# Moving the pool of split tiles behind the pool of small tiles, which changes its address modulo 512

## The chip, the cores and the metric

One core of one Trainium2 chip runs the whole program. The metric is the device time of one execution in microseconds, as the median of several runs.

## The reference

The program is a four-layer encoder on 256 tokens of width 1024, float32 throughout:

```python
for i in range(DEPTH):                        # 4 layers
    h = rmsnorm(x, norm_mix_g[i])
    h = mixer(h)                              # layer 0: SSD, 1: dilated attention, 2: differential attention, 3: SSD
    x = x + h
    x = x + jnp.square(jax.nn.relu(rmsnorm(x, norm_mlp_g[i]) @ w1[i])) @ w2[i]   # 1024 -> 4096 -> 1024
return rmsnorm(x, final_norm_g)
```

Nearly all the work is in products of the 256 tokens with weight matrices that are read once each (HBM reads are 296 MB in all).

## The kernel before, in words

**Products.** Activations lie transposed, 128 channels by 256 tokens to a tile. A product with weights is done at the fast matmul rate by splitting both factors: a hi part that is the float32 rounded to `float32r`, and a lo part, the rest. `mm3` (lines 144 to 151) then issues three matmuls into one place of PSUM. Each loads a 128x128 piece of weights into the array and streams an activation tile of 128x256 past it (the moving operand):

```python
mm(out, lhsT=wh, rhs=xh, start=start, stop=False, skip_group_check=True)   # L149
mm(out, lhsT=wh, rhs=xl, start=False, stop=False, skip_group_check=True)   # L150
mm(out, lhsT=wl, rhs=xh, start=False, stop=stop, skip_group_check=True)    # L151
```

A few weights stay whole (`native`); L147 multiplies them as plain float32 with the tile `nf`.

**Weights.** `pump` brings them in chunks of 128x1024: SP issues the DMA into `raw` (5 buffers), ScalarE copies the hi part into `whi` (L110), VectorE writes the rest into `wlo` (L112), 5 buffers each. The order of the chunks is planned ahead, and `done` lets the pump run on when TensorE is through with a chunk.

**Moving operands.** There are three families. `split_tile` (line 217) gives tiles `spl`, two 128x256 blocks each, from a ring of 12 in the pool `sp`; they outlive a layer and hold the split input of an MLP, of a mixer's first units (`norm_split`, L232 and L233) and the split inputs of the output projections. The tiles `nh` and `nl` (pool of the layer) hold the normalised input of a mixer, and `hh` and `hl` (pool of the layer) the hidden activations of an MLP.

**An MLP** (`mlp`, from line 325) goes over eight slices of 512 hidden channels. `up(s)` takes four chunks and multiplies them with all eight `spl` blocks, 96 matmuls into two `r` banks; `evac` squares and splits the result into `hh` and `hl`; `down(s - 1)` takes four chunks and multiplies them with `hh` and `hl`, 96 matmuls into the four `a` banks. `norm_finish` stands after the first `up`. So in each MLP 768 matmuls stream `spl` and 768 stream `hh` or `hl`, in turns of 96.

**The mixers** interleave their units by numbers in tables (`CFG`, `DIL`, `DIFF`). Their input projections stream `nh` and `nl`; the first units of each (`defer`) and all output chunks (`out_chunk`, `proj_tail`) stream `spl`. In the two SSD mixers these are 2 x 480 matmuls, in the dilated one 336, in the differential one 288. In the dilated mixer each pair of heads has two streams of `qk` (48 and 96 matmuls on `nh`) between its other work. In the differential mixer the V projection (L972 to L974) loads `nh` into the array and streams `whi` and `wlo`; its scores (L130, L131) load `q` and stream `k` and `kl`.

**Where things lie.** Pools are laid out one behind another in the order in which `Prog.__init__` makes them, each tile with its ring of buffers. Byte addresses in a partition of the built program:

| pool | tiles | begins | modulo 512 |
|---|---|---|---|
| `wp` | `raw`, then `whi`, then `wlo`, 5 x 4096 bytes each | 32032 (`whi` 52512, `wlo` 72992) | 288 |
| `sp` | 12 `spl` of 2048 bytes | 93472 | 288 |
| `small` | six of 32 bytes, nine of 1024 (`rbc`, `dg`, `sqacc`, `sq`): 9408 bytes | 118048 | `rbc` and later 480 |
| layer | `hh`, `hl`, or `nh`, `nl` first | 127456 | 480 (`nh`, `nl` of the dilated mixer 480 too) |

All buffers of `whi`, `wlo`, `spl`, `hh`, `nh` step by a multiple of 512 bytes, and a 128x128 piece of weights is 512 bytes wide, a moving block 1024; so all pieces of a family have the same address modulo 512. In the differential mixer `k` and `kl` begin at 0 modulo 512, and `q` too.

Of the kernel before, what the change touches and what calls it, by code (L numbers as in the profile page):

```python
# [35 lines left out]
class LayerPool:  # L36


    def __init__(self, prog):
        self.prog = prog  # L40
# [5 lines left out]
class Prog:  # L46
    def __init__(self, ctx, tc, aps, parts):
        self.ctx, self.tc, self.nc, self.a = ctx, tc, tc.nc, aps
        self.parts = parts
        ep = lambda name, bufs=1, **k: ctx.enter_context(tc.tile_pool(name=name, bufs=bufs, **k))  # L50
        self.const = ep("const")
        self.xp = ep("xp")
        self.wp = ep("wp")
        self.sp = ep("sp")
        self.ap_ = ep("small")
        self.lp = None
        self.dr = ep("dr", space=bass.MemoryType.DRAM)
        self.ps = ep("ps", space=PSUM)
        self.head = self.const.tile([P, aps["head"].shape[1]], F32, name="head")
        self.vec = self.const.tile([P, aps["vec"].shape[1]], F32, name="vec")  # L60
        self.cst = self.const.tile([P, aps["cst"].shape[1]], F32, name="cst")
        self.plan = []
        self.rep, self.bvec = {}, None
        self.n_dma = self.n_conv = self.n_take = self.n_done = 0
        self.chunks = {}
# [1206 lines left out]
```

## Time and profile before

| | |
|---|---|
| median of 3 runs | 1622.55 us (1619.86 to 1624.77) |
| the profiled execution | 1627.18 us, its span 1625.4 us |
| granted clock of TensorE, mean over the span | 0.987 |
| HBM read | 296.41 MB, 185 GB/s over the span |

The span lies between the first and the last instruction. A busy time of TensorE in the profile is the union of its matmuls' lengths; these overlap, so the length of one isn't what it costs. What it costs in a stream that does not wait is the step from its start to the start of the next, which the view of single instructions in order of time shows.

### The profile page before, as it was taken

Reading aid. Unit: us, or ns where it says so; the run is one execution under the profiler, and the core shown is the slowest. Engines: PE = TensorE matmul, PEld = TensorE weight load, DVE = VectorE, ACT = ScalarE, POOL = GpSimd, SP = SyncE. Lnnn points to the kernel's source line nnn. Section 1 sums busy time; section 2 is a strip of 40 time slices with the busy share of each in tenths; the row PEclk is TensorE's granted clock in tenths of the full one; section 3 lists DMA queues with packets and bytes.
Section 4 is the critical chain, followed back from the end, with each engine's and each line's share of the span. In section 5 each row is a group of like instructions: output and inputs, shape, how many; then the busy total and the mean of one; then the engine's idle time right before and its main releaser. Section 6 shows DMA issues by size and latency. Waiting matters only on the chain.

```text
span 1625.4 us, 32385 instructions
## 1 busy us (share of the span) xinstructions
PE 1594.5 (98%) x13018; PEld 1550.6 (95%) x13018; DVE 1194.8 (74%) x1996; ACT 959.2 (59%) x1627; POOL 132.9 (8%) x122
## 2 busy tenths in 40 slices
PE   8999999999999999999999999999999999999998
PEld 7989999999989999999999999999999899899997
DVE  6999997555777667666556898755579999985554
ACT  5577865444657666655445677544455777654443
POOL 0012121000200000010000100100010232210001
PEclk9999999999999999999999999999999999999999
DMA  6668755765465556546665564566656677656661
GB/s 209 220 211 240 227 193 178 222 211 184 137 179 161 168 156 170 170 141 184 186 191 183 177 200 133 179 193 184 187 144 199 210 218 222 212 174 184 193 184 64
DMA packets 230294, 299.84 MB, mean 184 GB/s; under 512 B 16496, under 2 KB 166256, under 8 KB 230144
## 3 DMA queue, kind: packets, MB, share of 16 engines
q1 hardware_dynamic: 209552, 262.51, 53.0%
q10 hardware_dynamic: 20592, 35.27, 7.5%
q8 instruction: 102, 1.67, 0.4%
q14 instruction: 48, 0.39, 0.1%
HBM read 296.41 MB, written 3.62 MB: 185 GB/s over the span
## 4 chain that ended last, share of the span: by engine, by line
PE 80%; DVE 10%; DMA 4%; ACT 3%; issue 2%; POOL 0%; SPq 0%; DVEq 0%; ACTq 0%; POOLq 0%
PE r L149 14%; PE r L151 14%; PE r L150 14%; PE a L149 8%; PE a L150 8%; PE a L151 8%; DVE wlo L112 3%; PE r L147 2%; DMA raw<-in_ssd_in_w_dram 2%; PE a L829 1%; PE a L828 1%; PE a L830 1%; DMA bc<-scr 1%; PE r L620 1%; PE a L887 1%
## 5 line engine op out<-in xcount | busy, mean ns | idle before, releaser
L112 DVE TENSOR_TENSOR wlo<-raw,whi 128x1024 fp32r<-128x1024 f32 (+1 forms) x490 | 592.1, 1216 | 307.2 <-ACT whi L110 306.7
L110 ACT CAST whi<-raw 128x1024 fp32r<-128x1024 f32 (+1 forms) x490 | 502.5, 1032 | 459.4 <-PE r L150 244.1
L151 PE MATMUL r<-spl,wlo 128*128 128x256 f32 x1248 | 357.4, 287 | 4.0 <-DVE wlo L112 4.0
L149 PE MATMUL r<-spl,whi 128*128 128x256 f32 x1248 | 359.0, 288 | 0.6 <-ACT whi L110 0.5
L150 PE MATMUL r<-spl,whi 128*128 128x256 f32 x1248 | 358.1, 287 | 0.3 <-DVE spl L233 0.3
L149 PE MATMUL r<-nh,whi 128*128 128x256 f32 (+1 forms) x1024 | 291.2, 284 | 5.4 <-DVE kl L142 3.7
L151 PE MATMUL r<-nh,wlo 128*128 128x256 f32 (+1 forms) x1024 | 285.9, 279 | 0.7 <-DVE wlo L112 0.7
L150 PE MATMUL r<-nl,whi 128*128 128x256 f32 (+1 forms) x1024 | 286.0, 279 | 0.0
L149 PE MATMUL a<-hh,whi 128*128 128x256 f32 x1024 | 283.3, 277 | 0.0
L150 PE MATMUL a<-hl,whi 128*128 128x256 f32 x1024 | 283.1, 276 | 0.0
L151 PE MATMUL a<-hh,wlo 128*128 128x256 f32 x1024 | 282.6, 276 | 0.0
L151 PEld LDWEIGHTS r<-spl,wlo 128*128 128x128 f32 x1248 | 243.0, 195 | 4.5 <-DVE wlo L112 4.4
L149 PEld LDWEIGHTS r<-spl,whi 128*128 128x128 f32 x1248 | 243.1, 195 | 1.3 <-ACT whi L110 1.0
L150 PEld LDWEIGHTS r<-spl,whi 128*128 128x128 f32 x1248 | 243.1, 195 | 0.9 <-DVE spl L233 0.5
L149 PEld LDWEIGHTS r<-nh,whi 128*128 128x128 f32 (+1 forms) x1024 | 193.0, 188 | 9.1 <-issue 5.4
L151 PEld LDWEIGHTS r<-nh,wlo 128*128 128x128 f32 (+1 forms) x1024 | 193.0, 188 | 1.7 <-DVE wlo L112 0.9
L150 PEld LDWEIGHTS r<-nl,whi 128*128 128x128 f32 (+1 forms) x1024 | 193.6, 189 | 0.7 <-DVE nl L306 0.2
L149 PEld LDWEIGHTS a<-hh,whi 128*128 128x128 f32 x1024 | 192.3, 188 | 0.2 <-ACT whi L110 0.2
L150 PEld LDWEIGHTS a<-hl,whi 128*128 128x128 f32 x1024 | 192.4, 188 | 0.0
L151 PEld LDWEIGHTS a<-hh,wlo 128*128 128x128 f32 x1024 | 192.2, 188 | 0.0
L246 POOL TENSOR_TENSOR sqacc<-sqacc,sq 128x256 f32<-128x256 f32 x48 | 43.0, 896 | 1111.6 <-ACT sq L244 1110.1
L595 ACT ACTIVATE e<-bc,tb 128x256 f32<-128x256 f32 (+1 forms) x256 | 95.5, 447 | 2.1 <-issue 1.7
(249 smaller groups left out, 2412.9 us busy)
## 6 DMA issues: line engine op xcount, KB each, us to landing
raw<-in_mlp_w_dram SPq DMA_DIRECT2D x256, 512.0 KB
raw<-in_ssd_in_w_dram SPq DMA_DIRECT2D x96, 512.0 KB
bc<-scr ACTq DMA_DIRECT2D x32, 768.0 KB
raw<-in_dil_qkv_w_dram SPq DMA_DIRECT2D x48, 512.0 KB
raw<-in_ssd_out_w_dram SPq DMA_DIRECT2D x32, 512.0 KB
raw<-in_dil_qkv_w_dram SPq DMA_DIRECT2D x64, 192.0 KB
raw<-in_diff_qkv_w_dram SPq DMA_DIRECT2D x24, 512.0 KB
raw<-in_dil_out_w_dram SPq DMA_DIRECT2D x8, 512.0 KB
```

Of the source, the lines that this page charges most:

```text
L110: self.nc.scalar.copy(out=hi[:, :n], in_=raw[:, :n])
L112: self.nc.vector.tensor_tensor(out=lo[:, :n], in0=raw[:, :n], in1=hi[:, :n].bitcast(F32), op=ALU.subtract)
L147: mm(out, lhsT=wh, rhs=xh, start=start, stop=stop, skip_group_check=True)
L149: mm(out, lhsT=wh, rhs=xh, start=start, stop=False, skip_group_check=True)
L150: mm(out, lhsT=wh, rhs=xl, start=False, stop=False, skip_group_check=True)
L151: mm(out, lhsT=wl, rhs=xh, start=False, stop=stop, skip_group_check=True)
L246: nc.gpsimd.tensor_tensor(out=self.sqs[0], in0=self.sqs[0], in1=sq, op=ALU.add)
L595: X = lambda o, i_, bias: nc.scalar.activation(out=o, in_=i_, func=AF.Exp, bias=bias)
L620: nc.tensor.matmul(b[(h % 2) * 64:(h % 2) * 64 + 64, n * T:(n + 1) * T], lhsT=xt[:, 1 - i, h * 64:(h + 1) * 64], rhs=G[h][:, i * T:(i + 1) ...
L828: mm(o, lhsT=nh[:, k, t], rhs=w_h, start=k == 0, stop=False)
L829: mm(o, lhsT=nh[:, k, t], rhs=w_l, start=False, stop=False)
L830: mm(o, lhsT=nl[:, k, t], rhs=w_h, start=False, stop=k == 7)
```

## The change

The pool `small` is made ahead of the pool `sp`, so it takes the place right behind the weights.

```diff
         self.wp = ep("wp")
+        self.ap_ = ep("small")
         self.sp = ep("sp")
-        self.ap_ = ep("small")
         self.lp = None
```

In the built program `small` now begins at 93472 and `sp` at 102880; everything else lies where it was. Each `spl` is 9408 bytes higher (18 x 512 + 192, so 480 modulo 512), each small tile 24576 bytes lower (48 x 512, the same modulo 512). The instructions of every engine, their order and what they wait for are the same in both programs, row by row.

## Rows read from the trace of the kernel before

**Rows 1.** Page, part 1: busy us of each engine (share of the span) xinstructions.

```profile
PE 1594.5 (98%) x13018; PEld 1550.6 (95%) x13018; DVE 1194.8 (74%) x1996; ACT 959.2 (59%) x1627; POOL 132.9 (8%) x122
```

**Rows 2.** Waits of PE, whole span, first and last row: us in total, times, longest.

```profile
PE r L151 <- DVE wlo L112: 4.7, 3, 3.7
...
PE r L149 <- DVE z L460: 0.2, 1, 0.2
```

**Rows 3.** Page, part 4: the chain that ended last, by engine.

```profile
PE 80%; DVE 10%; DMA 4%; ACT 3%; issue 2%; POOL 0%; SPq 0%; DVEq 0%; ACTq 0%; POOLq 0%
```

**Rows 4.** Waits of all engines from 269 to 427 us, an MLP.

```profile
ACT whi L110 <- PE r L150: 42.0, 23, 1.8
```

**Rows 5.** Groups by line and shape, engine PE: xcount | busy us, mean ns of one.

```profile
L151 PE MATMUL r<-spl,wlo 128*128 128x256 f32 x1248 | 357.4, 287 | 4.0 <-DVE wlo L112 4.0
L149 PE MATMUL r<-nh,whi 128*128 128x256 f32 x1008 | 286.5, 284 | 5.4 <-DVE kl L142 3.7 <-DVE cvx L475 1.4 <-DVE z L460 0.2
L149 PE MATMUL a<-hh,whi 128*128 128x256 f32 x1024 | 283.3, 277 | 0.0
...
L149 PE MATMUL a<-spl,whi 128*128 128x256 f32 x304 | 89.0, 293 | 0.0
```

**Rows 6.** PE in order of time, first MLP: start us, length. 87 and 93 steps.

```profile
372.39 0.28 PE L149 MATMUL r<-spl,whi 128*128 128x256 f32 x1
...
382.83 0.29 PE L149 MATMUL a<-hh,whi 128*128 128x256 f32 x1
...
383.19 0.28 PE L149 MATMUL a<-hh,whi 128*128 128x256 f32 x1
...
393.73 0.28 PE L149 MATMUL r<-spl,whi 128*128 128x256 f32 x1
```

**Rows 7.** PE in order of time, an output chunk of the first mixer, 20 steps.

```profile
199.44 0.28 PE L149 MATMUL a<-spl,whi 128*128 128x256 f32 x1
...
201.84 0.28 PE L151 MATMUL a<-spl,wlo 128*128 128x256 f32 x1
```

**Rows 8.** PE in order of time, V projection of the third mixer, 36 steps.

```profile
936.99 0.28 PE L972 MATMUL a<-whi,nh 128*128 128x256 f32 x1
...
941.07 0.28 PE L972 MATMUL a<-whi,nh 128*128 128x256 f32 x1
```

**Rows 9.** PE in order of time, scores of the third mixer, 6 steps.

```profile
934.36 0.28 PE L131 MATMUL r<-kl,q 128*128 128x256 f32 x1
...
935.08 0.29 PE L131 MATMUL r<-kl,q 128*128 128x256 f32 x1
```

**Rows 10.** Windows in six `nh` streams: busy (x) PE, PEld, DVE, ACT, POOL, PEclk, DMA.

```profile
505.50:514.50 9.00, 9.00 (x79) 9.00 (x78) 6.08 (x14) 6.36 (x14) 0.00 (x0) 1.00 0.36 103
537.00:546.00 9.00, 9.00 (x81) 9.00 (x81) 6.11 (x14) 6.38 (x14) 0.00 (x0) 1.00 0.37 99
568.20:577.20 9.00, 9.00 (x79) 9.00 (x78) 6.08 (x14) 6.37 (x14) 0.00 (x0) 1.00 0.35 100
599.80:608.80 9.00, 9.00 (x82) 9.00 (x81) 6.11 (x14) 6.38 (x14) 0.00 (x0) 1.00 0.38 108
631.00:640.00 9.00, 9.00 (x78) 9.00 (x78) 6.09 (x14) 6.37 (x14) 0.00 (x0) 1.00 0.35 101
662.50:671.50 9.00, 9.00 (x82) 9.00 (x81) 6.10 (x14) 6.37 (x14) 0.00 (x0) 1.00 0.38 118
```

**Rows 11.** PE in order of time, the long stream from 567 us, 93 steps.

```profile
567.40 0.28 PE L149 MATMUL r<-nh,whi 128*128 128x256 f32 x1
...
578.35 0.28 PE L130 MATMUL r<-q,q 128*128 128x256 f32 x1
```

**Rows 12.** PE in order of time, the last of six shorter streams, 45 steps.

```profile
653.46 0.28 PE L149 MATMUL r<-nh,whi 128*128 128x256 f32 x1
...
658.56 0.28 PE L130 MATMUL r<-q,q 128*128 128x256 f32 x1
```

**Rows 13.** Windows, from 1300 to 1350 us in the fourth mixer, columns as above.

```profile
1300.00:1350.00 50.00, 50.00 (x376) 45.99 (x375) 49.19 (x69) 36.74 (x72) 14.23 (x7) 1.00 0.78 240
```

## The prediction

> **What bounds the kernel now.** First the busy table: TensorE's matmuls fill 98% of the span, VectorE 74% [rows 1]. A busy share alone could hide waiting, so next the waits of TensorE. There are fourteen rows; the first is 4.7 us, the last 0.2 us, and all fourteen add up to 23 us, 1.4% of the span [rows 2]. The chain that ended last says the same, with 80% on TensorE [rows 3]. Inside an MLP the suppliers wait for TensorE: in the stretch from 269 to 427 us ScalarE's hi copy waited 42.0 us for a weight buffer that a matmul still read [rows 4], and TensorE has no row of its own there. So time taken out of TensorE's stream comes out of the span nearly whole.
>
> Then what one matmul costs. The groups give 287 ns for those that read `spl`, 277 for `hh`, 284 for `nh`, all of one shape [rows 5]. These are lengths of overlapping instructions; three are in flight at once, and 10 ns times 4656 would promise 47 us. The price is the step from one start to the next. In one MLP, 87 steps on `spl` take 10.44 us, which is **120.0 ns** a step, and 93 steps on `hh` take 10.54 us, which is **113.3 ns** [rows 6]. [...]
>
> Is it the address? In bytes modulo 512 the weights begin at 288, `spl` at 288 (distance 0), `hh` and `nh` at 480 (distance 192). Other differences are excluded one by one. The PSUM banks: an output chunk of the first mixer reads `spl` into the same rotating `a` banks in the same loop as `hh`, and takes 20 steps in 2.40 us, 120.0 ns [rows 7]. The converted weights: in the third mixer's V projection they are the moving operand, at 288, over loaded tiles at 480, and 36 steps take 4.08 us, 113.3 ns [rows 8]. The buffer: scores there have loaded and moving tiles both at 0, and 6 steps take 0.72 us, 120 ns [rows 9]. Wherever the distance is 0 the step is 120; at 192 either way it can be 113.
>
> It can be, but need not. The `nh` streams stand at the distance that `spl` gets, and there are two paces. Of six long streams in the second mixer, three hold 82, 82 and 81 matmuls in 9 us and three hold 79, 79 and 78, at the same clock [rows 10]. From first to last step the slow one is 93 in 10.95 us, **117.8 ns** [rows 11]; the quick one is the `hh` step. The six shorter streams between them are all quick, as the last of them, 45 steps in 5.10 us [rows 12]. A stream keeps its pace until something else interrupts it. I read this as a phase between weight load and moving read that the entry sets: by steps a third is slow (3 x 93 of 6 x 93 + 6 x 45), by streams 3 of 12.
>
> **The change part by part.** It adds, removes and moves no instruction, DMA or wait; queue orders are the same. The small tiles go down by 24576 bytes, 48 times 512, so their place modulo 512 stays: cost nothing, whatever modulo 512 does. `spl` goes up by 9408, which is 18 times 512 plus 192: its matmuls go from distance 0 to 192. That is 3 x (1248 + 304) = 4656 matmuls: 768 in each of four MLPs (3072), and in the mixers 1584, of which the two SSD mixers have 960.
>
> *An MLP.* Quick: 768 x (120.0 - 113.3) = 5.1 us gained. Slow: the 768 gain 2.2 ns each, 1.7 us; but `hh` follows `spl` without a pause. Today each `hh` stretch is entered from the 120 ns pace and finds the quick one. After the change both have one distance, nothing resets the pace, and the 768 `hh` steps would be slow too: 768 x 4.5 = 3.4 us lost, net 1.7 us slower. The pace is unknown, so I bound each MLP by -5.1 and +1.7 us and take three of four quick, as the nearest rows have it [rows 10, 12]: -15.3 + 1.7 = -13.6 us.
>
> *The mixers.* At two thirds quick a step gains 2/3 x 6.7 + 1/3 x 2.2 = 5.2 ns, times 1584 is 8.2 us. The output chunks there are 24 matmuls between other work and need some steps to settle; and in the SSD mixers VectorE is busy 49.19 of 50 us [rows 13], so part turns into waits for lo parts. I take three quarters, 6.1 us; the ends are 0 (VectorE hides all) and 10.6 us (all quick, all passed on).
>
> *What is late next.* In an MLP nothing: a chunk of weights takes TensorE 24 x 113.3 = 2.7 us, while one lo part takes VectorE 1.2 us, and the `hh` stretches already run at this rate without a wait.
>
> Sum: -13.6 - 6.1 = -19.7 us. The profiled execution took 1627.2 us (span 1625.4), 0.3% above the median of the three runs, 1622.55. Taken from the median: **1603 us**.
>
> [...] The rows show a step that follows distance [rows 6 to 9]. [...]
>
> **The rivals.**
> - *Nothing happens.* The two reads do not meet, and 120 belongs to something else that `spl` streams share, such as when their tiles are written. For it: only that the trace before has no `spl` at another distance. Against: rows 7 to 9. Time 1622.5. Chance 0.06.
> - *The slow pace takes the MLPs, and it ends slower.* Place: the first long run of an MLP after `norm_finish`, whose entry sets the pace for the next 180 us. Price: 1.7 us for each slow MLP, 5.1 us forgone. With q quick MLPs they yield 5.1q - 1.7(4 - q): nothing at q = 1, and a loss of 6.8 us at q = 0. If VectorE also hides what the mixers give, the time is 1629; if not, about 1626. For it: half of the long `nh` streams are slow. Against: the short ones, and `hh`. Chance of no quick MLP 0.04, of one 0.08 (time 1616).
> - *VectorE becomes the bound of the SSD mixers.* They give nothing, the MLPs stay: about 1607. This lies inside the forecast's range.
>
> **How the numbers follow.** My forecast, two or more quick MLPs, has 0.82: all four quick and the mixers' upper end give 1591.5, two quick about 1610. One quick gives 1616, and the range 1590 to 1618 takes it in; outside are mostly the rivals "nothing" and "none quick", 0.10, and whatever I did not see. About 0.3% (4.9 us) is what a measurement of this kernel can tell from no change. Faster by more: the forecast and most of one quick, 0.88. Within: "nothing" and a mixed rest, 0.09. Slower by more: no quick MLP with the mixers hidden, 0.03.
>
> **What would show it.** Right: in the profile after, steps on `spl` of 113 or 118 ns and none at 120 over a long stretch; `hh` and `spl` in one MLP at one pace; nearly no new row among TensorE's waits in the MLPs; the `nh` streams as mixed as now. Wrong: `spl` steps still at 120 (distance is not the cause); `hh` at 113 beside `spl` at 118 in one MLP (the pace is not carried over); or steps of 113 throughout with a span that hardly moves (waits for lo parts or DMAs took the gain).

## The result, and the profile after

The changed kernel takes 1610.06 us (median of 8 runs, 1605.08 to 1616.8) against 1626.24 us for the kernel before beside it: ratio 0.9906, interval 0.9882 to 0.993, 16.2 us faster by the medians. The forecast was 1603.0 us, 19.7 us below its base; the measured median lies inside its range. Two later sets gave 1611.88 against 1625.27 and 1605.67 against 1625.29. Over all 18 runs the change lies between 1603.0 and 1616.8 us, with a median of 1609.5.

The profiled run took 1616.8 us, the slowest of the 18. First its page, the busy line, the chain and three groups:

```profile
span 1615.0 us, 32385 instructions
...
PE 1579.2 (98%) x13018; PEld 1534.2 (95%) x13018; DVE 1193.0 (74%) x1996; ACT 959.2 (59%) x1627; POOL 133.1 (8%) x122
...
PE 75%; DVE 13%; DMA 5%; ACT 3%; issue 2%; POOL 0%; SPq 0%; DVEq 0%; ACTq 0%; POOLq 0%
...
L151 PE MATMUL r<-spl,wlo 128*128 128x256 f32 x1248 | 352.1, 282 | 3.7 <-DVE wlo L112 3.7
...
L149 PE MATMUL r<-nh,whi 128*128 128x256 f32 (+1 forms) x1024 | 291.6, 285 | 6.7 <-DVE kl L142 3.2
...
L149 PE MATMUL a<-hh,whi 128*128 128x256 f32 x1024 | 286.0, 279 | 0.0
```

TensorE is still 98% busy, with the same count [rows 1]; `spl` went from 287 to 282 ns, but `hh`, which nobody touched, from 277 to 279 [rows 5]. That is the first sign that `hh` lost something. In the chain TensorE lost five points, VectorE gained three and DMA one [rows 3].

The steps say more than the lengths. Next, single matmuls of TensorE in order of time (start us, length), the 96 on `spl` and the 96 on `hh` behind them, in the first MLP and then in the third:

```profile
351.03 0.28 PE L149 MATMUL r<-spl,whi 128*128 128x256 f32 x1
...
362.22 0.28 PE L151 MATMUL r<-spl,wlo 128*128 128x256 f32 x1
362.34 0.28 PE L149 MATMUL a<-hh,whi 128*128 128x256 f32 x1
...
373.53 0.28 PE L151 MATMUL a<-hh,wlo 128*128 128x256 f32 x1
...
1052.37 0.28 PE L149 MATMUL r<-spl,whi 128*128 128x256 f32 x1
...
1063.13 0.28 PE L151 MATMUL r<-spl,wlo 128*128 128x256 f32 x1
1063.25 0.28 PE L149 MATMUL a<-hh,whi 128*128 128x256 f32 x1
...
1074.01 0.28 PE L151 MATMUL a<-hh,wlo 128*128 128x256 f32 x1
```

In the first, 95 steps take 11.19 us, 117.8 ns a step, on `spl` and on `hh` alike. In the third they take 10.76 us, 113.3 ns, again on both. Before it was 120.0 and 113.3 [rows 6]. So one MLP keeps one pace throughout, and this run has both kinds. Windows of 40 us inside the four MLPs show which is which: the number behind the first x is the matmuls in the window, 40 us by the step and two or three that overlap its edges. The kernel before, one window (the others have x346, x346 and x344):

```profile
340.00:380.00 40.00, 40.00 (x346) 40.00 (x345) 21.53 (x21) 17.84 (x21) 0.00 (x0) 1.00 0.63 189
```

The changed kernel:

```profile
340.00:380.00 40.00, 40.00 (x342) 40.00 (x341) 21.67 (x21) 19.13 (x23) 0.00 (x0) 1.00 0.60 185
780.00:820.00 40.00, 40.00 (x342) 40.00 (x341) 22.76 (x23) 18.71 (x22) 0.00 (x0) 1.00 0.61 190
1080.00:1120.00 40.00, 40.00 (x355) 40.00 (x354) 23.35 (x23) 19.45 (x23) 0.00 (x0) 1.00 0.63 194
1490.00:1530.00 40.00, 40.00 (x356) 40.00 (x354) 23.40 (x23) 19.08 (x23) 0.00 (x0) 1.00 0.64 197
```

342 is an MLP at 117.8 ns, slower than before; 355 one at 113.3; 346 the old mixture of 120 and 113. Two MLPs of four were slow in this run. From the first to the last `hh` step an MLP took 157.4, 156.1, 156.1 and 158.4 us before, and now 159.6, 158.2, 152.2 and 154.5: +2.2, +2.1, -3.9, -3.9. That stretch holds 768 `hh` and 576 `spl` steps; by the steps it should be 768 x 4.5 - 576 x 2.2 = +2.2 and -576 x 6.7 = -3.9. The clock was 1.00 in all of these windows, before and after, so it is not the clock.

Waits of TensorE in the changed kernel, whole span (us in total, times, longest):

```profile
PE r L151 <- DVE wlo L112: 5.8, 2, 3.7
...
PE a L151 <- DVE wlo L112: 2.5, 1, 2.5
...
PE a L283 <- DVE dg L282: 1.3, 2, 0.6
...
PE r L587 <- ACT cb L579: 0.2, 1, 0.2
```

Seventeen rows, 28 us, where there were fourteen and 23 [rows 2]. From the first to the last `hh` step none lies inside an MLP: from 270 to 430 us, and in the same part of the other three, TensorE has no row, and ScalarE waits 40.8 us for it, much as before [rows 4]. Of the 5 us more, 1.3 us are a new row, two waits of L283 for `dg`: they belong to `norm_finish` and stand at the start of the second slice, in the first and in the last MLP. The rest is between the MLPs.

The `nh` streams are as mixed as before [rows 10]; the first two of the six long ones in the second mixer, in the changed kernel:

```profile
507.00:516.00 9.00, 9.00 (x78) 9.00 (x78) 6.09 (x14) 6.37 (x14) 0.00 (x0) 1.00 0.35 102
538.00:547.00 9.00, 9.00 (x81) 9.00 (x81) 6.33 (x13) 6.38 (x14) 0.00 (x0) 1.00 0.28 82
```

They are not mixed by chance: in all ten profiles of this model's kernels the first, third and fifth of the six are slow and the others quick.

### The profile page after: what moved, and what is told of

Read it like the earlier page. It is cut to its first block, busy times and chain, and to the rows that moved or that the text cites. A ratio compares the mean times of both kernels' runs of the same rounds, so it can differ in the third digit from the quotient of the medians.

```text
span 1615.0 us, 32385 instructions
## 1 busy us (share of the span) xinstructions
PE 1579.2 (98%) x13018; PEld 1534.2 (95%) x13018; DVE 1193.0 (74%) x1996; ACT 959.2 (59%) x1627; POOL 133.1 (8%) x122
## 4 chain that ended last, share of the span: by engine, by line
PE 75%; DVE 13%; DMA 5%; ACT 3%; issue 2%; POOL 0%; SPq 0%; DVEq 0%; ACTq 0%; POOLq 0%
PE r L149 13%; PE r L151 13%; PE r L150 13%; PE a L149 8%; PE a L150 8%; PE a L151 8%; DVE wlo L112 3%; DMA raw<-in_ssd_in_w_dram 2%; PE r L147 2%; DMA bc<-scr 1%; PE a L829 1%; PE a L830 1%; PE a L828 1%; PE r L620 1%; ACT whi L110 1%
## 5 line engine op out<-in xcount | busy, mean ns | idle before, releaser
L151 PE MATMUL r<-spl,wlo 128*128 128x256 f32 x1248 | 352.1, 282 | 3.7 <-DVE wlo L112 3.7
L149 PE MATMUL r<-spl,whi 128*128 128x256 f32 x1248 | 353.5, 283 | 0.5 <-ACT whi L110 0.5
L150 PE MATMUL r<-spl,whi 128*128 128x256 f32 x1248 | 353.2, 283 | 0.4
L151 PEld LDWEIGHTS r<-spl,wlo 128*128 128x128 f32 x1248 | 238.5, 191 | 4.3 <-DVE wlo L112 4.1
L150 PEld LDWEIGHTS r<-spl,whi 128*128 128x128 f32 x1248 | 239.1, 192 | 1.3 <-DVE spl L233 1.1
L149 PEld LDWEIGHTS r<-spl,whi 128*128 128x128 f32 x1248 | 238.7, 191 | 1.1 <-ACT whi L110 0.7
```

## The experiments

Theory A: the distance of the two addresses sets the step, and at 192 the entry of a stream chooses between two paces that it keeps. Theory B: the order of the pools, or what small tiles lie beside, matters in another way. Theory C: the pace belongs to something the streams share, not to addresses.

### 1. The order of the pools without the distance, and the distance without the order

```diff
# small_below_d0: the order of the change, but 192 bytes moved behind spl
+        self.ap_ = ep("small")
         self.sp = ep("sp")
-        self.ap_ = ep("small")
+        self.rp = ep("tiny")
...
-        t = lambda nm, dt=F32: self.ap_.tile(...)    # the six 32-byte tiles
+        t = lambda nm, dt=F32: self.rp.tile(...)
# rs_below_d192: the order of before, but those 192 bytes moved ahead of spl
         self.wp = ep("wp")
+        self.rp = ep("tiny")
         self.sp = ep("sp")
...
-        t = lambda nm, dt=F32: self.ap_.tile(...)
+        t = lambda nm, dt=F32: self.rp.tile(...)
```

In the first, `spl` lies 9216 bytes (18 x 512) further, at distance 0; in the second 192 bytes further, at 192.

> The small tiles lie below the split tiles as in the change, but the six tiles of 32 bytes (192 bytes in all) go above them, so that the split tiles keep distance 0 from the weights and the layer pool keeps 192. Theory of distance: steps on spl at 120.0 ns, time that of the kernel before, 1626 us within 0.3%. Rival (the order of the pools or the small tiles' place matters): the time after the change, 1605 to 1617 us.

> The order of the pools is that of before; only the six tiles of 32 bytes go below the split tiles, so that these begin 192 bytes further, and all else stays modulo 512. Theory of distance: steps on spl at 113 or 118 ns, whole MLPs at one pace, and times on the steps 1605, 1610 and 1616 us that the runs after the change show (each MLP that goes slow costs 5 to 7 us). Rival (order of the pools): the time before, 1626 us.

The first took 1625.05 us against 1626.72 (10 runs, ratio 0.9997, 0.9982 to 1.0012): nothing. The second took 1603.96 (4 runs, 1600.35 to 1613.72; ratio 0.9875, 0.9834 to 0.9917): the whole gain, and nominally more. The window in the first MLP, of the one with distance 0:

```profile
340.00:380.00 40.00, 40.00 (x346) 40.00 (x346) 22.40 (x22) 19.13 (x23) 0.00 (x0) 1.00 0.60 186
```

and of the one with distance 192, whose other three windows have x355 as well:

```profile
340.00:380.00 40.00, 40.00 (x355) 40.00 (x354) 21.38 (x22) 18.66 (x21) 0.00 (x0) 1.00 0.61 189
```

That settles B: the same order of pools gives 0 or 1% by 192 bytes alone. It also shows what the change can give when all four MLPs are quick: a span of 1603.0 us.

### 2. The step as a function of the distance

A program of streams alone, which computes nothing of the encoder: 16 moving tiles, each 32 bytes further than the one before (modulo 512), and for each six streams of 60 matmuls, entered behind a few short float32 matmuls of six lengths.

```python
mv = [c.tile([P, T + 8], F32R, name="mv" + "abcdefghijklmnop"[d]) for d in range(ND)]
...
for k in range(LEN):
    w = (wh, wh, wl)[k % 3]
    nc.tensor.matmul(b[:, 0:T], lhsT=w[:, q * P:(q + 1) * P], rhs=mv[d][:, 0:T], ...)
```

> No part of the model is computed: one program that only streams matmuls of the kernel's shape (128x128 loaded, 128x256 moving, float32r, hi, hi, lo in turn) at sixteen distances between moving operand and weights, 0 to 480 bytes modulo 512 in steps of 32 (tiles mva to mvp), six streams of 60 at each, with four short float32 matmuls between streams. Theory of distance: 120 ns a step at 0; at 192 113 ns in some streams and 118 in others, fixed for a stream once it has settled; other distances have paces of their own, some perhaps below 113. [...] Rival (the buffers differ, not the distance): no dependence on the distance here, since all sixteen tiles are written alike.

Mean of the last 30 steps of a stream, ns:

| distance | 0 | 32 | 64 | 96 | 128 | 160 | 192 | 224 |
|---|---|---|---|---|---|---|---|---|
| step | 120.0 | 116.5 to 116.7, or 117.8 | 117.8 | 120.0 | 118.7 | 117.3 or 118.7 | 113.3 or 117.8 | 118.3 |

From 256 to 480 the same values come again, stream by stream. Two streams at distance 192 (tile `mvg`, start us, length), the first and the last of 30 steps, the first pair quick and the second slow:

```profile
302.59 0.28 PE L44 MATMUL b<-mvg,wl 128*128 128x256 f32 x1
...
305.99 0.28 PE L44 MATMUL b<-mvg,wl 128*128 128x256 f32 x1
...
310.37 0.28 PE L44 MATMUL b<-mvg,wl 128*128 128x256 f32 x1
...
313.91 0.28 PE L44 MATMUL b<-mvg,wl 128*128 128x256 f32 x1
```

3.40 us and 3.54 us for the same instructions on the same addresses. Three of the six streams were quick, behind entries of 16, 64 and 112 columns, and at 448 the same three. So C falls: an address alone changes the step, with nothing else in the program. The map moves the moving tile alone; that the distance counts and not the tile's own address rests on the kernel before, where a moving tile at 288 modulo 512 is slow over weights at 288 (120.0 ns) and was quick over tiles at 480 (113.3) [rows 6, 8]. And "modulo 512" in the title of this case is too coarse: the pattern repeats every **256** bytes. Of the eight distances 192 is the only one that reached 113.3 here.

A second map took finer distances, and entered half of its streams behind 9, 12 or 24 matmuls at distance 0:

```diff
-                for k in range(4):
-                    nc.tensor.matmul(e[:, 0:ENTRY[s]], lhsT=ent, rhs=xin[:, 0, 0:ENTRY[s]], ...)
+                if s < 3:       # float32 matmuls of 16, 64, 128 columns, as above
+                else:           # 9, 12 or 24 matmuls of the stream's kind on a tile at distance 0
```

> No part of the model is computed: streams of 60 matmuls as in the first map, at sixteen other distances modulo 256 (192, 64, 32, 160, 176, 184, 188, 196, 200, 208, 216, 240, 8, 16, 48, 80 for mva to mvp), six at each: three entered from short float32 matmuls, three from 9, 12 or 24 matmuls at distance 0 without a pause. Phase theory: at 192 the streams entered from the pace of distance 0 all take 113.3 ns, as hh after spl did before the change, and those entered from float32 matmuls take 113.3 or 117.8. Rival (the entry does not matter, chance alone): the prefixed streams are as mixed as the others. Open: whether a distance that is no multiple of 32 gives a step below 113, or 113 alone.

At 192 all six were quick, but the trace shows them as four stretches and not six: the short matmuls of the first three ran together at the start, from 5.95 us, and the three streams follow as one run of 180 matmuls, behind 3 at distance 0; the others stand behind 6, 12 and 24. So none at 192 was entered from short matmuls here, and the comparison of the two entries is missing. What can be said is that four of four entered from distance 0 were quick, against six of twelve (192 and 448) entered from short matmuls in the first map. At other distances the entry does tell: at 8 the three behind short matmuls took 116.7 and the three behind distance 0 took 120.0. Around 192 the dip is narrow: 120.0 at 184, 188, 196 and 200, 119.1 to 119.3 at 176 and 208. The worst was 121.3 at 216, and nothing went below 113.3. At 64 one stream was quick and the others 117.8, and at 16 one was quick and the others 118.7, all three from distance 0 among the slow ones in both. So 192 is not the only distance that can reach 113.3. In the model's kernels 64 does so often: the V projection [rows 8], moving at 288 over tiles at 480, stands at 64 modulo 256 by the map's reckoning (288 - 480), and 21 of its 40 streams in the ten profiles are quick, the rest at 117.8.

### 3. What the mixers alone give, and where the pace comes from

64 bytes at the head of the MLP's pool put `hh` and `hl` at distance 0 modulo 256 (256 modulo 512) while `spl` keeps 192: the MLPs should cost what they did before, with the parts exchanged, and what is left is the mixers' gain.

```diff
         acc = [self.bank(f"a{i}") for i in range(4)]
+        self.lp.tile([P, 16], F32, name="gap")
```

> The change, and 64 bytes ahead of the hidden activations in the pool of each MLP, so that hh and hl begin 256 bytes from the weights. Phase theory with the period of 256 that the map showed: hh at 120.0 ns in all MLPs, and spl, now always entered from that pace, at 113.3 in all long stretches; an MLP costs what it did before the change, and the time is 1616 to 1623 us, the mixers' gain alone. Rival (period of 512): 256 has a pace of its own and hh is no slower than 118. Rival (carry-over is not what binds hh and spl): spl still at 118 in some MLPs.

1624.05 us (8 runs) against 1625.27, ratio 0.9989, interval 0.9974 to 1.0004. By the ratio the kernel gains **1.8 us**, between -0.6 and 4.2, just outside the 1616 to 1623 us that were expected. The window of the first MLP has nearly the old count, with the parts exchanged:

```profile
340.00:380.00 40.00, 40.00 (x344) 40.00 (x343) 22.81 (x23) 18.69 (x22) 0.00 (x0) 1.00 0.62 192
```

`hh` steps at 120 although its distance modulo 512 is 256: the shorter period holds in the kernel too. And all 24 runs of `spl` that follow `hh` here go at 113, as all 27 runs of `hh` that follow `spl` did in the kernel before. A stream at 192 that comes out of the 120 ns pace is quick, 51 times of 51; one that starts behind other work can be either.

The 1.8 us are not the mixers' gain alone, because the MLPs did not quite cost what they did before. From the first matmul of the first MLP's first slice to the start of its last `hh` matmul, in the kernel before and then here:

```profile
244.34 0.28 PE L149 MATMUL r<-spl,whi 128*128 128x256 f32 x1
...
426.90 0.28 PE L151 MATMUL a<-hh,wlo 128*128 128x256 f32 x1
...
247.07 0.28 PE L149 MATMUL r<-spl,whi 128*128 128x256 f32 x1
...
431.15 0.28 PE L151 MATMUL a<-hh,wlo 128*128 128x256 f32 x1
```

That is 182.6 us and 184.1; over the four MLPs this one is 1.5, 0.3, 0.9 and 0.6 us longer, 3.3 in all. From the first to the last `hh` step the four lost 4.6 us, for 768 steps got slower there and 576 quicker. The 192 `spl` steps of each ahead of that should have given 5.1 us back and gave 1.3: two of the four entries were slow, and the waits for `dg` stand there. If the MLPs of its other runs cost the same, the mixers' gain is 1.8 + 3.3 = 5.1 us, between 2.7 and 7.5 (an estimate). The same division of the other profiles, in us:

| kernel | `spl` at | slow MLPs | four MLPs | all else | span |
|---|---|---|---|---|---|
| before | 0 | | 728.0 | 897.4 | 1625.4 |
| `small_below_d0` | 0 | | 728.0 | 895.1 | 1623.1 |
| the change, three profiles | 192 | 2, 1, 1 | 722.9, 716.9, 716.8 | 892.1, 894.8, 888.7 | 1615.0, 1611.7, 1605.5 |
| `rs_below_d192` | 192 | 0 | 710.4 | 892.6 | 1603.0 |
| `hh_d0` | 192 | `spl` entry slow in 2 | 731.3 | 890.7 | 1622.0 |

Outside the MLPs the means are 896.2 us at distance 0 and 891.8 at 192, 4.5 us apart, with single runs 3 us to either side.

### 4. Forcing the quick pace

If coming out of the 120 ns pace is what makes a stream at 192 quick, a few matmuls at distance 0 inside an MLP would make the rest of it quick. A copy of two of the eight `spl` blocks at distance 256, read in the second and fourth slices (24 matmuls each), should do it; a copy at distance 192, with the same extra work, should not.

```diff
# twin_d0, on top of the change; twin_d192 leaves out the line with gap, and gap2 has 64
+        self.lp.tile([P, 16], F32, name="gap")
+        twin = [self.lp.tile([P, 2, T], F32R, name=n) for n in ("twinh", "twinl")]
+        self.lp.tile([P, 48], F32, name="gap2")
+        for k in (2, 3):
+            nc.scalar.copy(out=twin[0][:, k - 2, :], in_=self.uh[k].bitcast(F32))
+            nc.vector.tensor_copy(out=twin[1][:, k - 2, :], in_=self.ul[k].bitcast(F32))
...
+                    xh, xl = (twin[0][:, kk, :], twin[1][:, kk, :]) if j == 1 and s in (1, 3) else (self.uh[k], self.ul[k])
-                                 self.uh[k], self.ul[k], k == 0 and n % 2 == 0, k == 7)
+                                 xh, xl, k == 0 and n % 2 == 0, k == 7)
```

> The change, and in each MLP copies (twin) of two of the split blocks that lie at distance 0 from the weights; the slices 1 and 3 of up read these for their second chunk, 24 matmuls, the first of them right behind the last pause of the MLP's start. Phase theory: the 24 take 120 ns each (0.16 us more), and the stream behind them goes at 113.3 ns to the end of its MLP, in all four MLPs and in every run, so the times lie at the fast end of what the runs after the change show, 1600 to 1606 us, without those of 1609 to 1617. Rival (the pace of an MLP is chance, or is set by something else than the entry): slow MLPs as often as before, times spread from 1600 to 1617 us.

> As twin_d0, with the same copies at distance 192, so that nothing at distance 0 stands at the MLP's start. Phase theory: some MLPs at 117.8 ns, times spread from 1600 to 1617 us as after the change. Rival (the copies themselves help): the times of twin_d0.

> The changed kernel itself on the same chip, to have more of its runs beside the others. Phase theory: times in groups some 5 to 7 us apart, one group for each number of slow MLPs, between 1600 and 1617 us.

The copy at 256 took 1608.85 us (6 runs, 1606.11 to 1611.73), ratio 0.9897 (0.9876 to 0.9919); the copy at 192 took 1607.46 (4 runs, 1601.59 to 1611.47), 0.9886 (0.9859 to 0.9914); the change itself 1611.88 (4 runs, 1605.4 to 1616.38), 0.9913 (0.9885 to 0.9942). By time the three are not told apart, and the copy at 256 missed the 1600 to 1606 us that were expected of it. By pace they go as expected as far as they go: with the copy at 256 all four MLPs were quick; with the copy at 192 the first began at 117.8 and became quick only behind its bias work at 295 us, the other three were quick from the start; in the change the third was slow. The copies also cost a little: at the start of the first and the last MLP the step to L283, which waits for `dg` on VectorE, is 1.08 and 1.23 us where the change has 0.92 and 0.91.

So a cheaper one: one block only, both copies on ScalarE, read in the second slice (12 matmuls) and in the first MLP in the fourth too, behind its bias work.

```diff
-        twin = [self.lp.tile([P, 2, T], F32R, name=n) for n in ("twinh", "twinl")]
-        self.lp.tile([P, 48], F32, name="gap2")
-        for k in (2, 3):
-            nc.scalar.copy(out=twin[0][:, k - 2, :], in_=self.uh[k].bitcast(F32))
-            nc.vector.tensor_copy(out=twin[1][:, k - 2, :], in_=self.ul[k].bitcast(F32))
+        twin = [self.lp.tile([P, T], F32R, name=n) for n in ("twinh", "twinl")]
+        self.lp.tile([P, 112], F32, name="gap2")
+        for t, x in zip(twin, (self.uh[2], self.ul[2])):
+            nc.scalar.copy(out=t, in_=x.bitcast(F32))
...
+                    xh, xl = twin if k == 2 and (s == 1 or s == 3 and l == 0) else (self.uh[k], self.ul[k])
```

> As twin_d0 with one block copied instead of two, by ScalarE alone, and read in slice 1 of each MLP (in the first MLP in slice 3 too, behind its bias work): 12 matmuls at distance 0, one of them ahead of the start's last pause. Phase theory: the four MLPs quick in the profile; without VectorE's copies the 1.2 us wait for dg goes, and the time is 1601 to 1606 us, some 5 us below the change's. Rival (the copies' cost eats what the quick MLPs give): 1607 to 1611 us, no better than the change.

> The changed kernel once more beside twin_one on the same chip. Both theories: 1605 to 1617 us; its profile shows which of its MLPs are slow, and phase theory expects another set than the two profiles so far.

It took 1605.28 us (4 runs, 1602.74 to 1607.08), ratio 0.9874 (0.9856 to 0.9891), and the change beside it 1605.67 (6 runs, 1603.01 to 1611.94), 0.9881 (0.986 to 0.9902). The expected other set of slow MLPs did not come: the change had the same one slow as the time before. Windows of the second and third MLP, first of the kernel with the copied block (its other two have x356 and x355):

```profile
780.00:820.00 40.00, 40.00 (x355) 40.00 (x354) 22.60 (x23) 19.78 (x23) 0.00 (x0) 1.00 0.63 191
1080.00:1120.00 40.00, 40.00 (x356) 40.00 (x355) 21.72 (x22) 17.32 (x20) 0.00 (x0) 1.00 0.61 196
```

and of the change in that set:

```profile
780.00:820.00 40.00, 40.00 (x356) 40.00 (x355) 21.73 (x22) 17.53 (x19) 0.00 (x0) 1.00 0.63 197
1080.00:1120.00 40.00, 40.00 (x342) 40.00 (x341) 20.86 (x20) 17.17 (x19) 0.00 (x0) 1.00 0.58 186
```

With the copies at 256 eight MLPs of eight were quick. Without a copy at distance 0 seven of 24 entries were slow (two, one and one in the change, none with the tiny pool below, two with `hh` at 0, one with the copy at 192), so eight quick ones by luck would come about one time in sixteen, if the entries were independent draws. They are not: in the second and third MLP, 11 of 12 entries without a copy kept across `norm_finish` the pace of the `spl` steps ahead of it, and the fourth MLP was never slow. What the copy does is better seen there. In six of its eight MLPs the steps ahead of `norm_finish` were slow, and behind the copied block they were quick; the third MLP of the last kernel, 20 steps ahead and 47 behind:

```profile
1021.26 0.28 PE L149 MATMUL r<-spl,whi 128*128 128x256 f32 x1
...
1023.62 0.28 PE L151 MATMUL r<-spl,wlo 128*128 128x256 f32 x1
...
1026.48 0.28 PE L149 MATMUL r<-spl,whi 128*128 128x256 f32 x1
...
1031.81 0.28 PE L151 MATMUL r<-spl,wlo 128*128 128x256 f32 x1
```

118.0 ns a step and then 113.4. In the second and third MLP, of slow stretches ahead, all three turned quick with the copy, and one of five without it. These are small numbers, and it is the 51 of 51 that carry it. What it is worth in time isn't settled: the medians of this last pair differ by 0.4 us, while the change's 18 runs reach up to 1616.8 and the four of the copied block only to 1607.1.

## Why the prediction was right, and where it was off

- **The distance sets the step: right.** All rivals without it fell (experiments 1 and 2). "Nothing happens" had supposed reads that do not meet, so that a distance is worth nothing; the map shows 113.3 or 117.8 ns a step at 192 against 120.0 at 0, for identical instructions on other addresses. "At 192 either way" joined two distances, 192 and 64; both have the two paces in the kernels.
- **Two paces, kept for a whole MLP, with `hh` drawn along: right,** and this was the part that a sum from `spl` alone would have missed. The sizes were a little large. From the first matmul of an MLP to its last `hh` start a quick one gave 3.9 to 4.9 us where 5.1 was forecast, and a slow one cost 1.8 to 2.2 where 1.7 was. The stretch measured above goes by the steps (3.9 and -2.2); the 192 `spl` steps ahead of it should have added 1.3 in a quick MLP and added 0.1 to 1.1, least in the first and the last MLP, where TensorE waits for `dg`. With three quick MLPs the four gave 11.1 us, not 13.6.
- **Three of four quick: right as a mean, wrong for the profiled run, and partly luck.** Slow were two, one and one in the three profiles of the change. Of 24 entries without a forced pace seven were slow, near the third that was assumed. But that third had come from streams [rows 10, 12] of which the same three are slow in every profile, so it was no frequency, and the pace of an MLP is often older than the place that the prediction named: it passes through `norm_finish`. The sum has no single value: each slow MLP costs 6.1 to 6.7 us against a quick one, and the profiled run of 1616.8 us had two, while the tiny pool's, with none, took 1604.84. No profile had fewer than two quick MLPs.
- **The mixers' 6.1 us: near, within what the runs can tell.** The profiles give 4.5 us, the control of experiment 3 about 5.1. With 11.1 from the MLPs the profiles' sum is 15.6 us, and the three sets gave 16.2, 13.4 and 19.6.
- **Nothing late in an MLP: right but for the waits for `dg`. In the mixers the third rival came in part,** and not where I looked. I had put VectorE's limit on the fourth mixer [rows 13]; it is the first that gave nothing. Its `spl` steps got shorter, but the first `hh` step came at 270.5, 271.5, 271.7, 271.1 and 272.4 us in the five profiles at 192 without copies, against 269.5 and 271.9 in the two at 0. The wait for one lo part there was 2.0 to 2.2 us in all eight profiles at 192, and 0.7 and 1.7 in the two at 0.

One of those pauses, in the changed kernel. VectorE in order of time: the lo part that TensorE waits for, the first of the two from 184.97 us, stands behind a product of 2.33 us and other work, and VectorE has no gap.

```profile
179.65 1.21 DVE L112 TENSOR_TENSOR wlo<-raw,whi 128x1024 fp32r<-128x1024 f32 x1
180.79 2.33 DVE L608 TENSOR_TENSOR G<-e,cb 128x1024 f32<-128x1024 f32 x1
183.04 0.87 DVE L645 SCALAR_TENSOR_TENSOR spl<-t,vec,spl 128x256 fp32r<-128x256 f32 x2
183.83 1.21 DVE L570 TENSOR_TENSOR bc<-bc,cst 128x1024 f32<-128x1024 f32 x1
184.97 2.34 DVE L112 TENSOR_TENSOR wlo<-raw,whi 128x1024 fp32r<-128x1024 f32 x2
```

TensorE at the end of it, with the wait in brackets, and the step behind it:

```profile
186.23 0.58 PE L151 MATMUL r<-nh,wlo 128*128 128x256 f32 x1 [2.17 <-DVE wlo L112]
186.61 0.42 PE L149 MATMUL r<-nh,whi 128*128 128x256 f32 x1
186.82 0.42 PE L150 MATMUL r<-nl,whi 128*128 128x256 f32 x1
```

Windows ahead of, behind and well behind the pause (PEclk is the third number from the end):

```profile
182.00:185.90 3.90, 2.06 (x19) 1.86 (x17) 3.90 (x5) 3.90 (x7) 0.03 (x1) 1.00 0.38 140
186.10:189.40 3.30, 3.17 (x15) 3.17 (x16) 3.30 (x8) 2.81 (x7) 0.00 (x0) 0.50 0.60 156
189.60:193.00 3.40, 3.40 (x32) 3.40 (x31) 3.40 (x6) 2.47 (x5) 0.00 (x0) 1.00 0.57 171
```

and the middle one in the kernel before:

```profile
186.10:189.40 3.30, 3.30 (x30) 3.30 (x30) 3.30 (x10) 0.64 (x3) 0.00 (x0) 1.00 0.91 285
```

Behind the wait of 2.17 us the granted clock is 0.50, and 15 matmuls go where 30 went: a further 1.6 us. TensorE had been busy 2.06 of the 3.90 us ahead of it. A dip of this kind stands near 187 or near 237 us in all eight profiles with `spl` at 192, and in neither with `spl` at 0. The wait alone doesn't decide it: five of the eight had a wait of 2.0 to 2.2 us on the same lo part without a dip behind it (theirs stands near 237 us, behind a wait of 1.1 to 1.3 us), and with the small tiles below at distance 0 there was one of 1.7 us, without a dip.

Still open: what in the entry chooses the pace (both paces came from the same addresses and instructions), why 192 modulo 256 of all distances is the good one, and why the first mixer keeps nothing of its quicker steps. Only addresses and entries were varied, so no run here shows whether or where the two reads meet, or the phase between them that the prediction read into the two paces.

## What to carry to other kernels

Price a dense stream by the step from start to start, and when two families of equal matmuls differ, compare where their moving operand lies against the loaded weights: here 120.0 ns at distance 0 and, in its quick pace, 113.3 at 192 modulo 256, for a few bytes of padding ahead of a pool. Then ask who follows without a pause, because a pace was handed on here: the family that was already quick can lose what the other gains (`hh` went from 113.3 to 117.8 ns in the slow MLPs). And see whether the suppliers of a quicker TensorE have room; in the first mixer it met VectorE's full queue and waited, in the profiled run 2.17 us, with a granted clock of 0.50 behind the wait. Last, measure a control's other parts too: the kernel that was to show the mixers alone had also made its MLPs 3.3 us longer.

## What the runs showed that was not expected

- The pattern repeats every 256 bytes, not 512: stream by stream in the map, and `hh` at 256 steps at 120 as at 0.
- The good distance is narrow: 113.3 ns at 192, 120.0 four bytes to either side.
- For a stream at 192, coming out of one at distance 0 is a good entry: 51 of 51 were quick, while MLP entries behind other work were slow seven times in 24. The kernel before got its quick `hh` from its slow `spl`. It is no general rule: at 64 and at 16 none of three entered from distance 0 was quick.
- A pace outlasts a short interruption: in the second and third MLP it passed through `norm_finish` 11 times of 12.
